# A hybrid RWKV-7 and convolution block: other waits, buffers, sums and lags in a planned order of work

## The chip, the cores and the metric

The kernel runs on one core of a Trainium2 chip. The metric is device time in microseconds; before the change the median of three runs is 1135.36 us (1134.06 to 1135.81). TensorE does the matrix products, ScalarE (ACT) activations and evictions from PSUM, VectorE (DVE) elementwise work, GpSimd (POOL) here mostly issues transfers, and SyncE (SP) issues the others.

## What is computed

One layer on 512 tokens with 1024 channels, all in float32. The input x is normalised and goes through one wide projection; its columns feed two branches, which are gated and merged, projected, and added to x; a gated feed-forward layer of width 2816 follows.

```python
h = rms_norm(x, pre_mix_norm); proj = h @ w_in
p_r, p_k, p_v, p_c, z_rwkv, z_conv = split(proj)
y_rwkv = rwkv7_time_mix(...)      # per token and head, S is 64x64:
#   sa = S a_t;  S = S * w_t + sa b_t' + v_t k_t';  y_t = S r_t
#   then a norm over each head, a bonus term, a gate and @ w_rwkv_out
y_conv = conformer_conv(p_c, ...) # u * sigmoid(gate), a causal depthwise
#   convolution of 31 taps, layer_norm, silu, @ w_conv_out
merged = sigmoid(z_rwkv) * y_rwkv + sigmoid(z_conv) * y_conv
x = x + rms_norm(merged @ w_out)
f = (silu(h2 @ ffn_w_gate) * (h2 @ ffn_w_up)) @ ffn_w_down
x = x + rms_norm(f)
```

## The kernel before

Channels lie on the 128 partitions, in eight tiles (ct = 0 to 7, two heads each), and the 512 tokens along the free dimension. Float32 products are made from two rounded parts: each factor is split into a high and a low part, and `acc3` makes three matmuls of 512 columns for each 128x128 block (high by high, high by low, low by high). A dense tile of the projection is 8 such blocks, 24 matmuls, in two halves of four blocks.

The weights of a half are loaded by `wload` (L437). In the usual way SP loads wf, ACT makes wh and DVE subtracts to get wl. In the way used during the time mixing, `eng is G`, GpSimd loads wh, ACT writes wl = -wh, and a second GpSimd transfer adds the weights to wl while it writes (`accum_op`), so that wl holds what the rounding left out. wh and wl share twelve buffers, that is six halves.

The time mixing is cut into 8 chunks of 64 tokens. For each tile four generators run, with their priorities: `prep` (2), `values` (2), `chain` (0), and `taps` (5); `solve` and `finish` are started by prep and chain (3).

- `prep(ct)` makes the keys, waits for inner(ct-1) and chain(ct-2), writes AR and bk, transposes bk, then waits for solve(ct-1) (L832) and makes the products gps between them, of which Mt is evicted. Then it posts inner(ct) and starts solve(ct).
- `solve(ct)` inverts the triangular 64x64 matrices in Mt: blocks of 16 on DVE (tt, Ps), and then the products wqs, xqs, wps and xps on TensorE. Its result goes into Pbd, of which there are two (ct % 2).
- `values(ct)` waits for the dense tile v and writes UV and SV (product vps), then the bonus (product bps), and posts val(ct). vps, bps and the four products of solve share one PSUM buffer, tag "sb", in the order in which they ask for it.
- `chain(ct)` waits for chain(ct-1), val(ct) and solve(ct), and goes through the 8 chunks in sequence: zt from AR and SV, eviction zs on ACT, zt from Pbd and zs, two evictions UV, zt from bkT and UV, two evictions SV, and the next chunk.
- `taps(ct)` adds the 31 taps of the convolution into csum_ on DVE, each operation reading the sum that the one before wrote (L1057).

The order on each engine is written by a planner, `Sched`, while the program is built. Every operation is put into a queue of its engine and stream, with its inputs, priority and estimated duration (`times`). `run` takes the operation that can start earliest by the planner's clocks; among those that can start within EPS = 0.15 us of that, the one of lowest priority number. `after` (L272) says when a result may be used on another engine: its end plus LAG of the engine that makes it. A generator that yields an event goes on when that event's operations have been issued in the plan. Dense tiles are the filler (priority 4); `feed` loads at most WB = 6 halves ahead, and each tile of the projection has events that it needs: v of tile ct needs val(ct-1), the convolution's columns from tile 5 on need inner(ct-1), the gates z_conv need inner(7) and val(7). The engines themselves run in order and wait only for semaphores, so an operation that the plan places late isn't run earlier, and a DMA whose buffer is free may be issued before the plan's time.

After the eighth chain come the output projections, the convolution's norm, the merge and the feed-forward layer; from the projection w_out on the order is that of the code, without the planner.

Of the kernel before, what the change touches and what calls it, by code (L numbers as in the profile page):

```python
# [9 lines left out]
F32 = mybir.dt.float32  # L10
F32R = mybir.dt.float32r
I32 = mybir.dt.int32
AF = mybir.ActivationFunctionType
ALU = mybir.AluOpType
# [3 lines left out]
P = 128  # L18
T = 512
# [4 lines left out]
NCH = T // L  # L24
# [5 lines left out]
KW = 31  # L30
# [2 lines left out]
WT = 4  # L33
LB = {"mu_r": 2, "mu_k": 2, "mu_v": 1}
NWO = 3
BUFS = (2, 2, 2, 2, 1, 1, 1)
EPS = 0.15
C0 = math.exp(-0.5)
RSQ = float(0x5F3759DF)
# [42 lines left out]
def tile_hybrid_block(ctx, tc, xT, cst, prm, dwp, wl1, w2g, w_in, w_ro, w_co, w_o,  # L82
# [13 lines left out]
    class Sched:  # L96
# [7 lines left out]


        ENGS = ("PE", "ACT", "DVE", "POOL", "SP")
        LAG = {"PE": 0.06, "ACT": 0.07, "DVE": 0.06, "POOL": 0.1, "SP": 0.1}

        def __init__(self):
            self.cur, self.pri, self.seq = None, 0, 0  # L110
# [71 lines left out]
        def times(self, eng, name, k, aps):  # L182

            out = aps[0]
            n = math.prod(out.shape[1:])
            if eng == "PE":
                lhsT, rhs = k["lhsT"], k["rhs"]
                n, m = math.prod(rhs.shape[1:]), math.prod(lhsT.shape[1:])
                if lhsT.dtype == F32R:
                    c = max(0.112, 0.452e-3 * n)  # L190
                elif name == "transpose":
                    c = 0.112
                elif m > 64:
                    c = 2 * (0.112 if n <= P else 1.02e-3 * n) * (0.52 if lhsT.shape[0] <= 64 else 1)
                else:
                    c = 0.058 if m > 32 else 0.016
                return c, c + 0.17, 0.0
            if "dma" in name:
                size = P * n * 4 if out.shape[0] > 64 else 64 * n * 4
                land = 2.0 + size / 200e3  # L200
                if eng == "POOL":
                    return (0.91, 0.06, land + 0.7) if k.get("accum_op") else (0.65, 0.06, land + 0.3)
                return 0.06, 0.06, land
            psum = any(str(a.space) == "PSUM" for a in aps[1:])
            if eng == "ACT":
                t = 0.17 + 0.9e-3 * n - (0.03 if psum else 0)
                t += sum(0.08 for a in ("scale", "bias") if hasattr(k.get(a), "ap"))
                return t + 0.02, t, 0.0
            if eng == "POOL":
                return 0.2 + 1.2e-3 * n, 0.2 + 1.2e-3 * n, 0.0  # L210
            t = 0.16 + 1.035e-3 * n
            if name == "scalar_tensor_tensor":
                t += 0.05 if n > 64 else 0
            elif name == "transpose":
                t = 0.16 + 1.8e-3 * n
            elif name == "tensor_tensor_scan":
                t = 0.16 + 2.06e-3 * n
            elif name in ("tensor_scalar", "tensor_copy"):
                t = 0.15 + 0.75e-3 * n
            return t - 0.08, t, 0.0  # L220
# [139 lines left out]
    sc = Sched()  # L360
# [18 lines left out]
    V, G, S = Engine("DVE", nc.vector), Engine("POOL", nc.gpsimd), Engine("ACT", nc.scalar)  # L379
    PE, SY = Engine("PE", nc.tensor), Engine("SP", nc.sync)  # L380
# [17 lines left out]
    def f(ap):  # L398
        return ap.bitcast(F32)
# [17 lines left out]
    def vec(name, ct, lo=0, hi=P):  # L417
        j = VECS.index(name) * NT + ct
        return pr[lo:hi, j:j + 1]
# [17 lines left out]
    def wload(wap, nk, eng=None):  # L437
        if eng is G:
            wh, wl = (wp.tile([P, nk * P], F32R, tag=f"w{next(turn) % 3}", name=n_)
                      for n_ in ("wh", "wl"))  # L440
            G.dma_start(out=wh, in_=wap)
            S.activation(out=wl, in_=f(wh), func=AF.Copy, scale=-1.0)
            with sc.stream("low"):
                G.dma_start(out=wl, in_=wap, accum_op=ALU.add)
        else:
            wf = wp.tile([P, nk * P], F32, tag="w0", name="wf")
            wh, wl = (wp.tile([P, nk * P], F32R, tag=f"w{i}", name=n_)
                      for i, n_ in ((1, "wh"), (2, "wl")))
            SY.dma_start(out=wf, in_=wap)
            split(wf, wh, wl)  # L450
        return wh, wl
# [78 lines left out]
    cpad0 = hp.tile([P, KW - 1 + T], F32, tag="cpad0", bufs=1, name="cpad0")  # L530
    G.memset(cpad0[:, 0:KW - 1], 0.0)
    csum_ = hp.tile([P, KW - 1 + T], F32, tag="cpad1", bufs=1, name="cacc")
# [32 lines left out]
    for k in range(NT):  # L565
        if k == WK:
# [4 lines left out]
                               op0=ALU.mult, op1=ALU.subtract)  # L571
# [11 lines left out]
    def normed():  # L583
        for k in range(NT):
# [7 lines left out]
                    op0=ALU.mult, op1=ALU.add)  # L592
# [3 lines left out]
                    op0=ALU.mult, op1=ALU.add)  # L596
# [3 lines left out]
    Pbd = []  # L600
    kp = None
# [71 lines left out]
    def open_loop():  # L673
        nonlocal kp
        ctx_e.close()
        kp = pool(ctx_w, "kp", 2)
        for j in range(2):
            t_ = kp.tile([P, NCH, P], F32, tag=f"Pbd{j}", bufs=1, name=f"Pbd{j}")
            G.memset(t_, 0.0)
            Pbd.append(t_)  # L680

    def ktmp(name, bufs=1, cols=T):
        pool = kp if name in ("mu_v", "ep") else kq
# [61 lines left out]
    def once(fn):  # L745
        fn()
        yield from ()


    def prep(ct):  # L750
# [9 lines left out]
        for R, c in ((E, slice(0, P)), (O, slice(P, 2 * P))):  # L760
# [8 lines left out]
                             op0=ALU.mult, op1=ALU.add)  # L769
# [29 lines left out]
                               op0=ALU.mult, op1=ALU.mult)  # L799
# [18 lines left out]
        for hc in range(2):  # L818
            ps = pm.tile([P, 4, P], F32, tag="sm", name="tps")
            for c in range(4):  # L820
# [6 lines left out]
                               op0=ALU.mult, op1=ALU.mult)  # L827
        sc.post(("tr", ct))


        if ct:
            yield ("solve", ct - 1)  # L832
        Mt = kp.tile([P, NCH, L], F32, tag="Mt", bufs=BUFS[4], name="Mt")
        GR = kp.tile([P, NCH, 2, L], F32, tag="GR", bufs=BUFS[1], name="GR")
        sm = lambda rows: m_str[rows].unsqueeze(1).to_broadcast([64, 4, L])
        for hc in range(2):
# [6 lines left out]
            for par, ps in enumerate(pss):  # L843
# [3 lines left out]
                             func=AF.Copy)  # L847
                S.activation(out=Mt[r0 + B32:r0 + L, cc, 0:B32],
                             in_=ps[r0 + B32:r0 + L, :, B32:L], func=AF.Copy)
# [3 lines left out]
        s_.update(AR=AR, GR=GR, bkT=bkT, dL=dL)  # L853
        sc.post(("inner", ct))
        s_.update(Mt=Mt)
        sc.spawn(once(lambda: solve(ct)), 3)

    def solve(ct):
        s_ = st[ct]
# [4 lines left out]
                    in_=Mt[:, :, 0:B32].rearrange("p c t -> p t c").unsqueeze(2)  # L864
# [7 lines left out]
        for j in range(B16 - 1, 0, -1):  # L872
            q0 = j // 4
            n = 4 - q0
# [6 lines left out]
                    in_=Ps[:, 0:B32 * 8].rearrange("p (i q) -> p q i", q=8))  # L881
# [28 lines left out]
                          start=True, stop=True)  # L910
        for h in range(2):
            S.activation(out=Wt[R2[h]], in_=ps[R2[h]], func=AF.Copy)
        pb = Pbd[ct % 2]
        for h in range(2):
            for j, R in enumerate((R1[h], R2[h])):
                S.activation(out=pb[R, :, h * L + j * B32:h * L + (j + 1) * B32], in_=P32[R],
# [111 lines left out]
    conv_in = {}  # L1028

    def conv_place(ct):  # L1030
        if "ca" not in acts:
            acts["ca"] = hp.tile([P, NT, KW - 1 + T], F32, tag="ca", name="ca")
            G.memset(acts["ca"][:, :, 0:KW - 1], 0.0)
        return acts["ca"][:, ct, :]
# [22 lines left out]
    def taps(ct):  # L1057
        tap = lambda j: dw[:, ct * KW + j:ct * KW + j + 1]
        yield ("cv", ct)
        if ct:  # L1060
            yield ("taps", ct - 1)
        else:
            yield "low1"
        cb, o_ = conv_in[ct], csum_[:, 0:T]
        V.tensor_scalar(out=o_, in0=cb[:, 0:T], scalar1=tap(0), scalar2=vec("conv_b", ct),
                        op0=ALU.mult, op1=ALU.add)
        for j in range(1, KW):
            to = o_ if j < KW - 1 else conv_place(ct)[:, KW - 1:]
            V.scalar_tensor_tensor(out=to, in0=cb[:, j:j + T], scalar=tap(j), in1=o_,
                                   op0=ALU.mult, op1=ALU.add)  # L1070
        sc.post(("taps", ct))
        if ct == NT - 1:
            sc.fast = False
# [380 lines left out]
```

## Time and profile before

| | |
|---|---|
| runs | 1135.81, 1134.06, 1135.36 us |
| profiled execution | 1134.7 us, span 1132.9 us |
| granted clock of TensorE, mean | 0.974 |
| busy: TensorE, DVE, ACT, POOL | 1080.3, 745.1, 573.8, 106.0 us |
| dense matmuls, name dn, from 75 to 530 us | 887, 256.0 us busy |
| chain that ended last, on PE | 84% of the span |

The span runs from the first to the last instruction of the profiled execution. Busy times are unions of the instructions of an engine. Matmuls are pipelined and their modelled lengths overlap, so the step from one to the next is read from the start times. The granted clock is a share: 1.00 is 2.4 GHz, 0.50 is 1.2 GHz.

### The profile page before, as it was taken

To read this page: it belongs to the slowest core of one execution; us is meant where nothing else is said; L and a number is where in the kernel's file an instruction comes from. 1 tells how busy PE (TensorE), PEld (TensorE's weight loads), DVE (VectorE), ACT (ScalarE), POOL (GpSimd) and SP (SyncE) were. 2 spreads that over 40 slices of the span, in tenths; PEclk is the share of its full clock that TensorE was granted. 3 is DMA by queue.
4 is the path that set the end of the run, shared out by engine and by line. 5 is a ranking of instruction groups with operands and counts; after the bars stand their busy time and mean duration, and the time that the engine had idled before them with its cause. 6 is when DMAs were issued, how large, how long until landed. Compare 5 with 4: busy or idle time off the path is not lost.

```text
span 1132.9 us, 18576 instructions
## 1 busy us (share of the span) xinstructions
PE 1080.3 (95%) x7066; PEld 865.5 (76%) x7066; DVE 745.1 (66%) x1503; ACT 573.8 (51%) x1199; POOL 106.0 (9%) x175
## 2 busy tenths in 40 slices
PE   7799999998999999979999999999999999999996
PEld 5587777776676777757878888898888888888886
DVE  5878989898888898988855257375444444433324
ACT  5556677777666676545366235453333333333321
POOL 0013322131231221110000000000000000000000
PEclk9899999999998999969999999999999999999998
DMA  6117755262545344343322225401222222333312
GB/s 235 38 38 149 150 110 115 54 128 45 109 74 121 74 108 78 76 68 114 107 84 96 93 93 168 130 1 56 94 93 93 93 95 97 96 96 103 113 53 75
DMA packets 69017, 108.01 MB, mean 95 GB/s; under 512 B 15168, under 2 KB 20672, under 8 KB 68928
## 3 DMA queue, kind: packets, MB, share of 16 engines
q1 hardware_dynamic: 48768, 70.11, 19.8%
q0 software_dynamic: 20160, 36.71, 16.3%
q8 instruction: 56, 0.92, 0.3%
q14 instruction: 33, 0.27, 0.1%
HBM read 102.60 MB, written 2.10 MB: 92 GB/s over the span
## 4 chain that ended last, share of the span: by engine, by line
PE 84%; issue 7%; DVE 4%; ACT 2%; DMA 1%; POOL 1%; SPq 0%; DVEq 0%; POOLq 0%; ACTq 0%
PE dn L225 35%; PE dn L300 29%; PE zt L300 5%; PE lora L300 2%; PE psf L225 2%; PE gps L300 2%; PE wo L225 2%; PE yp L300 1%; PE vps L300 1%; PE psn L225 1%; PE tps L300 1%; POOL wl L300 1%; ACT Mt L300 1%; PE ssy L300 1%; POOL wh L300 0%
## 5 line engine op out<-in xcount | busy, mean ns | idle before, releaser
L225 ACT ACTIVATE wh<-wf 128x512 fp32r<-128x512 f32 x140 | 86.7, 619 | 217.8 <-PE dn L225 207.3
L225 DVE TENSOR_TENSOR wl<-wf,wh 128x512 fp32r<-128x512 f32 x140 | 94.2, 674 | 123.8 <-ACT wh L225 123.7
L300 PE MATMUL dn<-HH,wl 128*128 128x512 f32 x408 | 167.9, 412 | 3.0 <-DMA wl<-in_w_in_dram 3.0
L300 PE MATMUL dn<-HL,wh 128*128 128x512 f32 x408 | 168.4, 413 | 0.0
L300 PE MATMUL dn<-HH,wh 128*128 128x512 f32 x408 | 167.7, 411 | 0.0
L300 DVE SCALAR_TENSOR_TENSOR cacc<-ca,dw,cacc 128x512 f32<-128x512 f32 x203 | 151.9, 748 | 4.9
L225 PE MATMUL dn<-FHH,wl 128*128 128x512 f32 x320 | 127.7, 399 | 0.0
L225 PE MATMUL dn<-FHL,wh 128*128 128x512 f32 x320 | 126.2, 394 | 0.0
L225 PE MATMUL dn<-FHH,wh 128*128 128x512 f32 x320 | 125.5, 392 | 0.0
L225 PE MATMUL dn<-FH,wh 128*128 128x512 f32 (+1 forms) x332 | 101.3, 388 | 0.0
L300 PEld LDWEIGHTS dn<-HH,wl 128*128 128x128 f32 x408 | 78.2, 192 | 17.7 <-DMA wl<-in_w_in_dram 3.6
L300 PEld LDWEIGHTS dn<-HH,wh 128*128 128x128 f32 x408 | 78.1, 192 | 14.4 <-issue 0.2
L300 PEld LDWEIGHTS dn<-HL,wh 128*128 128x128 f32 x408 | 78.1, 191 | 14.2 <-issue 0.5
L300 POOL DMA_DIRECT2D wl<-in_w_in_dram x70 | 61.8, 931 | 262.9 <-ACT wl L300 188.4
L300 ACT ACTIVATE wh<-wf 128x512 fp32r<-128x512 f32 x68 | 42.3, 628 | 74.0 <-PE dn L300 69.4
L225 PEld LDWEIGHTS dn<-FH,wh 128*128 128x128 f32 x332 | 61.5, 188 | 13.9
L225 PEld LDWEIGHTS dn<-FHL,wh 128*128 128x128 f32 x320 | 60.1, 188 | 15.6
L300 DVE TENSOR_TENSOR wl<-wf,wh 128x512 fp32r<-128x512 f32 x68 | 46.5, 688 | 38.2 <-ACT wh L300 38.0
L225 PEld LDWEIGHTS dn<-FHH,wh 128*128 128x128 f32 x320 | 60.1, 188 | 14.3
L225 PEld LDWEIGHTS dn<-FHH,wl 128*128 128x128 f32 x320 | 60.1, 188 | 13.7
L225 PE MATMUL dn<-FH,wl 128*128 128x512 f32 (+1 forms) x166 | 64.0, 385 | 0.0
L300 POOL DMA_DIRECT2D wh<-in_w_in_dram x70 | 45.6, 718 | 36.9 <-PE dn L300 36.1
(304 smaller groups left out, 2078.6 us busy)
## 6 DMA issues: line engine op xcount, KB each, us to landing
wh<-in_w_in_dram POOLq DMA_DIRECT2D x70, 256.0 KB, 5.1
wl<-in_w_in_dram POOLq DMA_DIRECT2D x70, 256.0 KB, 4.4
wf<-in_w_gt_dram SPq DMA_DIRECT2D x44, 256.0 KB, 2.7
wf<-in_w_up_dram SPq DMA_DIRECT2D x44, 256.0 KB, 2.6
wf<-in_w_in_dram SPq DMA_DIRECT2D x42, 256.0 KB, 2.9
wf<-in_w_dn_dram SPq DMA_DIRECT2D x40, 256.0 KB, 2.7
wf<-in_w_ro_dram SPq DMA_DIRECT2D x16, 256.0 KB, 2.6
wf<-in_w_co_dram SPq DMA_DIRECT2D x16, 256.0 KB, 2.7
```

Source lines behind the costliest of these rows:

```text
L225: return fn(*a, **k)
L300: i = fn(*a, **k)
```

## The change

It has five parts, all in the stretch that the planner orders.

1. The planner's lags grow: 0.15 us behind an operation of PE, ACT and DVE (0.06, 0.07 and 0.06 before) and 0.2 behind POOL (0.1). Elementwise work on POOL is priced at 0.2 us + 2 ns an element of a partition instead of 1.2 ns.
2. Mt has two buffers instead of one, and the products gps of tile ct wait for solve(ct-2) instead of solve(ct-1).
3. Pbd has one buffer instead of two. solve becomes a generator: after wps it waits for chain(ct-1), and then writes Pbd and makes xps.
4. In `wload` the negation wl = -wh moves from ACT to GpSimd, into the stream "low" beside the accumulating transfer.
5. For tiles 1 to 7 the taps go by turns into two sums, csum_ and cpad0 (the input of tile 0's convolution, not used after that), and one addition joins them.

```diff
-BUFS = (2, 2, 2, 2, 1, 1, 1)
+BUFS = (2, 2, 2, 2, 2, 1, 1)
...
-        LAG = {"PE": 0.06, "ACT": 0.07, "DVE": 0.06, "POOL": 0.1, "SP": 0.1}
+        LAG = {"PE": 0.15, "ACT": 0.15, "DVE": 0.15, "POOL": 0.2, "SP": 0.1}
...
             if eng == "POOL":
-                return 0.2 + 1.2e-3 * n, 0.2 + 1.2e-3 * n, 0.0
+                return 0.2 + 2e-3 * n, 0.2 + 2e-3 * n, 0.0
...
             G.dma_start(out=wh, in_=wap)
-            S.activation(out=wl, in_=f(wh), func=AF.Copy, scale=-1.0)
             with sc.stream("low"):
+                G.tensor_scalar(out=wl, in0=f(wh), scalar1=-1.0, scalar2=None, op0=ALU.mult)
                 G.dma_start(out=wl, in_=wap, accum_op=ALU.add)
...
-        for j in range(2):
-            t_ = kp.tile([P, NCH, P], F32, tag=f"Pbd{j}", bufs=1, name=f"Pbd{j}")
-            G.memset(t_, 0.0)
-            Pbd.append(t_)
+        t_ = kp.tile([P, NCH, P], F32, tag="Pbd", bufs=1, name="Pbd")
+        G.memset(t_, 0.0)
+        Pbd.append(t_)
...
-        if ct:
-            yield ("solve", ct - 1)
+        if ct > 1:
+            yield ("solve", ct - 2)
...
-        sc.spawn(once(lambda: solve(ct)), 3)
+        sc.spawn(solve(ct), 3)
...
-        pb = Pbd[ct % 2]
+        if ct:
+            yield ("chain", ct - 1)
+        pb = Pbd[0]
...
-        cb, o_ = conv_in[ct], csum_[:, 0:T]
-        V.tensor_scalar(out=o_, in0=cb[:, 0:T], scalar1=tap(0), scalar2=vec("conv_b", ct),
+        cb = conv_in[ct]
+        sums = [t_[:, 0:T] for t_ in ((csum_, cpad0) if ct else (csum_,))]
+        n = len(sums)
+        V.tensor_scalar(out=sums[0], in0=cb[:, 0:T], scalar1=tap(0), scalar2=vec("conv_b", ct),
                         op0=ALU.mult, op1=ALU.add)
-        for j in range(1, KW):
-            to = o_ if j < KW - 1 else conv_place(ct)[:, KW - 1:]
-            V.scalar_tensor_tensor(out=to, in0=cb[:, j:j + T], scalar=tap(j), in1=o_,
-                                   op0=ALU.mult, op1=ALU.add)
+        if n > 1:
+            V.tensor_scalar_mul(sums[1], cb[:, 1:1 + T], tap(1))
+        for j in range(n, KW):
+            V.scalar_tensor_tensor(out=sums[j % n] if j < KW - 1 or n > 1 else
+                                   conv_place(ct)[:, KW - 1:], in0=cb[:, j:j + T],
+                                   scalar=tap(j), in1=sums[j % n], op0=ALU.mult, op1=ALU.add)
+        if n > 1:
+            V.tensor_add(conv_place(ct)[:, KW - 1:], *sums)
```

## Rows read from the trace of the kernel before

**Rows 1.** The page, part 1: busy us (share of the span) and instructions.
```profile
PE 1080.3 (95%) x7066; PEld 865.5 (76%) x7066; DVE 745.1 (66%) x1503; ACT 573.8 (51%) x1199; POOL 106.0 (9%) x175
```

**Rows 2.** Stretches: length, busy us and count by engine, granted clock, DMA share, GB/s.
```profile
75.00:530.00 455.00, 429.33 (x4024) 331.60 (x4023) 397.94 (x921) 301.87 (x751) 102.52 (x161) 0.95 0.46 95
...
100.00:275.00 175.00, 171.50 (x1741) 133.35 (x1740) 158.88 (x393) 122.88 (x300) 43.83 (x69) 1.00 0.50 102
275.00:400.00 125.00, 114.23 (x1047) 88.93 (x1048) 108.24 (x236) 83.70 (x207) 30.62 (x49) 0.92 0.48 101
...
475.00:525.00 50.00, 40.98 (x244) 30.44 (x243) 39.42 (x66) 28.32 (x76) 5.18 (x6) 0.80 0.32 65
525.00:1133.00 608.00, 596.40 (x2832) 491.00 (x2830) 299.37 (x515) 231.95 (x386) 0.00 (x0) 0.99 0.30 93
```

**Rows 3.** The seven stretches at a clock of 0.50 to 0.51, summed, by engine.
```profile
sum 41.10, PE 36.56 PEld 29.71 DVE 32.20 ACT 20.45 POOL 8.37; mean PE 5.22 PEld 4.24 DVE 4.60 ACT 2.92 POOL 1.20
```

**Rows 4.** The same seven stretches, the instructions of tile dn alone.
```profile
sum 41.10, PE 11.37 PEld 7.14 DVE 0.00 ACT 0.00; mean PE 1.62 PEld 1.02 DVE 0.00 ACT 0.00
```

**Rows 5.** A stretch of dense matmuls alone, at full clock.
```profile
600.00:625.00 25.00, 25.00 (x109) 20.17 (x108) 12.25 (x20) 14.33 (x21) 0.00 (x0) 1.00 0.32 108
```

**Rows 6.** Timeline of PE, 355 to 361 us: start, us, engine, line, operation, idle before.
```profile
356.46 0.49 PE L300 MATMUL zt<-SV,AR 128*128 128x128 f32 x2 [0.36 <-ACT SV L300]
...
359.80 0.49 PE L300 MATMUL zt<-SV,AR 128*128 128x128 f32 x2 [0.72 <-ACT SV L300]
```

**Rows 7.** Tile zt, who waited for it: us in all, times.
```profile
  PE zt L300: 13.3, 24
```

**Rows 8.** Timeline of ACT, 338 to 348 us: the last copies into Pbd.
```profile
345.67 0.76 ACT L300 ACTIVATE Pbd<-xps 32x256 f32<-32x256 f32 x2
```

**Rows 9.** Timeline of PE, 338 to 348 us: the products gps of the next tile.
```profile
346.69 0.48 PE L300 MATMUL gps<-AR,bk 64*128 64x128 f32 x2
```

**Rows 10.** Tile Pbd: durations in ns, least, median and most; first and last start.
```profile
L300 ACT ACTIVATE Pbd<-P x32: 397/415/417, 126.3 to 475.5; 32x256 f32<-32x256 f32 x32
L300 ACT ACTIVATE Pbd<-xps x16: 373/375/377, 128.6 to 478.8; 32x256 f32<-32x256 f32 x16
L300 POOL MEMSET Pbd<- x2: 962/962/962, 67.1 to 68.0; 128x1024 f32 x2
```

**Rows 11.** Timeline of ACT, 470 to 486 us: the last v tile's eviction.
```profile
476.50 0.69 ACT L300 ACTIVATE mu_v<-dn,drv 128x512 f32<-128x512 f32 x1
```

**Rows 12.** Timeline of PE, 476 to 496 us: values, bonus, first dense matmul after them.
```profile
481.03 2.08 PE L300 MATMUL vps<-cs,mu_v 128*128 128x128 f32 x8
...
490.99 0.77 PE L300 MATMUL dn<-HH,wh 128*128 128x512 f32 x1
```

**Rows 13.** Groups by line and shape: count, busy us, mean ns, idle before.
```profile
L300 ACT ACTIVATE wl<-wh 128x512 fp32r<-128x512 f32 x70 | 43.3, 627 | 1.8 <-DMA wh<-in_w_in_dram 0.6
```

**Rows 14.** Timeline of POOL, 455 to 496 us.
```profile
458.12 3.22 POOL L300 DMA_DIRECT2D wh<-in_w_in_dram  x6
491.07 0.89 POOL L300 DMA_DIRECT2D wl<-in_w_in_dram  x1 [29.73 <-ACT wl L300]
```

**Rows 15.** Waits of PE: for whom, us in all, times, longest.
```profile
PE dn L300 <- DMA wl<-in_w_in_dram: 3.0, 2, 2.3
```

**Rows 16.** Timeline, 494 to 504 us: eight taps on DVE without a break.
```profile
493.91 6.26 DVE L300 SCALAR_TENSOR_TENSOR cacc<-ca,dw,cacc 128x512 f32<-128x512 f32 x8
```

**Rows 17.** Timeline of DVE, 67 to 70 us: two operations that don't read each other.
```profile
68.71 0.75 DVE L300 SCALAR_TENSOR_TENSOR mu_k<-dn,pr,mu_k 128x511 f32<-128x511 f32 x1
69.37 0.68 DVE L300 TENSOR_TENSOR wl<-wf,wh 128x512 fp32r<-128x512 f32 x1
```

**Rows 18.** Tile cacc: the first tap, durations in ns.
```profile
L300 DVE TENSOR_SCALAR cacc<-ca,dw,pr x7: 541/545/546, 137.5 to 504.7; 128x512 f32<-128x512 f32 x7
```

**Rows 19.** Timeline of ACT, 576 to 584 us: the normed convolution, first tile.
```profile
582.74 0.62 ACT L300 ACTIVATE CH<-ca 128x512 fp32r<-128x512 f32 x1
```

**Rows 20.** Timeline of PE, 650 to 656 us: the first matmul that reads it.
```profile
652.71 0.40 PE L300 MATMUL dn<-CH,wh 128*128 128x512 f32 x1
```

## The prediction

> **What bounds the kernel now.** I read the page's shares first: TensorE is busy 1080.3 us, 95% of the span of 1132.9 [rows 1]. Then I cut the span into stretches, to see where the other 52 us lie and at what clock [rows 2]. After 525 us some 12 us of 608 are idle, at a granted clock of 0.99: the end of the kernel is TensorE work that this change does not touch. From 75 to 530 us, in the part that the planner orders, TensorE is busy 429.3 of 455.0, so 25.7 us are idle, at a mean clock of 0.95. By parts, 100 to 275 us has 3.5 us idle; 275 to 400 us has 10.8 (clock 0.92), and 475 to 525 us has 9.0 (clock 0.80). TensorE is the limit while it has dense work, and loses time where the recurrence alone may run.
>
> The clock is the second loss. Seven short stretches, 41.1 us together, ran at 0.50, the lower level of 1.2 GHz, each behind an idle time. TensorE is busy 36.6 us in them, 11.4 of it in dense matmuls [rows 3, 4]. A dense matmul takes 0.229 us at the higher level (25.00 us for 109) [rows 5] and twice that at the lower, so half of the 11.4 is lost, 5.7 us. Of the other 25.2 busy us between none and half is the clock's; I take a quarter, 6. So about 12 us (6 to 18) go with the clock. Idle time and clock together are 37 us (32 to 44), and that is all that another order can win in this stretch.
>
> DVE comes next: 397.9 us of the 455, 87%; in 100 to 275 us it is 158.88 of 175, 91%. ACT has 301.9 (66%), POOL 102.5 (23%) [rows 2].
>
> **The change part by part.** The profiled execution took 1134.7 us, 1.8 more than its span and 0.7 less than the median of 1135.36; the sum is made against 1134.7.
>
> *Margin (LAG).* One step of the recurrence without dense work takes 3.34 us, from zt at 356.46 to zt at 359.80 us [rows 6]. By the prices and lags in its code the planner sets 3.04 us for these six hops (PE 0.45, zs 0.33, PE 0.45, UV 0.49, two products 0.68, SV 0.65, lags included); the new lags add three times 0.09 and three times 0.08 and make it 3.55. So the old plan calls a step ready 0.3 us early, and TensorE, which works in order, stands there; the new one is 0.2 late, and dense matmuls fill that. All that TensorE's matmuls wait for evictions of zt and of what follows it is 13.3 us, 24 times [rows 7], partly where no dense matmul is at hand, as in the step of [rows 6]. So margin alone wins between 0 and 8 us, and may lose 3 by starting late what could start; I take a win of 2.
>
> *Second Mt, one Pbd, the new waits.* With two buffers for Mt the products gps of tile ct need no finished solve(ct-1). In tile 5 this wait decides: the last copies of solve(4) start at 345.67 and take 0.76, and gps follows at 346.69 [rows 8, 9]. In exchange solve(ct) writes its result only after chain(ct-1): four copies of 0.415 us, then two of 0.375 [rows 10], 2.4 us on ACT, ahead of the first product with it. Queued behind them on ACT are the next chain's evictions and the prep of the tile after. Where that is late, it costs 2.4 us a tile in 7 tiles, 17 us; where the preceding chain ends before the values are ready, nothing. The new wait also turns the order on the one PSUM buffer "sb": the values' product vps stood behind xps of the same tile, and may now come ahead of it. This matters most at the end: mu_v of the last tile is evicted at 476.50, vps starts at 481.03, and only when the values are done may the next gate tiles be loaded; the first dense matmul follows at 490.99 [rows 11, 12]. In the 50 us around it TensorE loses 9.0 us idle and some 6 by clock. I take 7 of these 15 as won, and 6 of the 16 in 275 to 400 us (10.8 idle, 5 by clock). The ends are all 31 won, and 17 lost.
>
> *Negation on GpSimd.* ACT loses 70 activations, 43.3 us [rows 13], 14% of its work in the stretch. That is off the path, but it ends a wait: POOL issues six wh loads from 458.12 us on, and then stands 29.73 us for ACT's copy, which lies far back in ACT's order, until wl's DMA at 491.07 [rows 14]. TensorE's own wait for wl is 3.0 us [rows 15]; it goes, and is counted in the idle time above. What one negation takes on POOL no row shows. Below it lies half of the 0.962 us memset of 1024 columns, 0.48; above it one such memset for reading and writing 512 columns and a wait for a whole tap of 0.75, 1.7 [rows 10, 16]. I take 1.0, nearer to the memset. POOL then has 102.5 + 70 = 172 us (136 to 222) of 455. Behind the negation in POOL's queue stand the wl DMA of the same half and the wh DMAs of the halves that follow; with over half of POOL idle they come no later than they are used.
>
> *Taps in two sums.* Eight taps in a row take 6.26 us, 0.783 each; two operations that don't read each other start 0.66 apart (68.71 and 69.37) [rows 16, 17]. Per tile 0.545 + 30 x 0.783 = 24.0 us become 2 x 0.545 + 29 x 0.66 + 0.68 = 20.9 (0.545 is the first tap's [rows 18], 0.68 the TENSOR_TENSOR's of [rows 17]): 3.1 us by seven tiles, 22 us where all follow each other, some 12 where a part lies between other work. TensorE gets nothing from it: the first CH made from the taps is written at 582.74 and read at 652.71 us, 70 us later [rows 19, 20].
>
> *DVE against GpSimd.* POOL's two memsets [rows 10] only write, and POOL has no operation that reads SBUF, so the trace leaves open whether a negation and a tap can run together. If not, DVE pays 70 x 0.48 to 0.96, 34 to 67 us; if they can, nothing. I take 15, about what the two sums return, and so no cost on the path. The Trainium skill ("SBUF — State Buffer", section "SBUF: two separate sides") speaks against the change here: a DVE operation with two SBUF inputs and a GpSimd operation that reads SBUF take one port pair in turn, each for its whole length. No run here shows it yet. By that rule the 34 to 67 would be paid, and the first rival below is what that makes of the time.
>
> Sum: 1134.7 - 2 - 7 - 6 = 1119.7, and at the level of the median 1120.
>
> **The rivals.**
> *GpSimd stops DVE (slower).* DVE has 398 + 50 (the middle of 34 to 67) - 15 = 433 us. It decides from 413 us on, 91% of the 455, the highest share in [rows 2]. At that share 433 us need 476, 21 more than now, less some 6 that TensorE still wins: 1150 (1138 to 1165). For: DVE is 87% full, and most of its work there reads two tensors. Against: the taps may end 70 us later before anybody waits for them.
> *The starvation stays (no change).* The gates' loads still wait for the values of the last tile, the recurrence still runs alone at 475 to 525 us, and a new order loses elsewhere what it wins: 1128 to 1137. For: the waits in the code that hold these loads back are the same. Against: the order on "sb" and the wait for solve are what make the values late.
> *One Pbd makes the chains wait (slower).* 17 us, less 3 won: 1149. It decides if solves are early and the chains follow each other at once. Against: the copies of solve(4) are followed by gps, not by the chain [rows 8, 9], so the values are what chains wait for.
> *All of it goes.* Idle time and half-speed stretches vanish but for a few us: 1100 (1095 to 1106).
>
> **How the numbers follow.** My forecast, 1106 to 1129, gets 0.49; GpSimd against DVE 0.21; no change 0.17; one Pbd 0.07; all of it 0.06. 0.2% is 2.3 us, about what a measurement of this kernel can tell from no change. Of the no-change case 0.09 falls within it, 0.06 is faster, 0.02 slower. So faster is 0.49 + 0.06 + 0.06 = 0.61, same 0.09, slower 0.21 + 0.07 + 0.02 = 0.30. For 8 in 10 the range reaches from 1101 to 1151: left out are half of the two slow cases, 0.14, and half of the fastest, 0.03. The likeliest case's own range is 1106 to 1129.
>
> **What would show it.** The margin: TensorE's waits behind zt below 10 us in all. The new waits: under 6 us idle in 275 to 400 us, and the last chain with dense matmuls between its steps and the clock at its higher level. POOL: wl's DMAs a few us behind the landing of wh, and no wait of 20 us for them. The sums: taps 0.66 apart. Against me: taps of 1 us and more beside negations, negations far above 1 us, or DVE over 413 us in the stretch; a chain that starts right behind Pbd's copies while TensorE idles; a new idle stretch of TensorE at another place.

## The result, and the profile after

The changed kernel takes 1142.0 us (median of four runs, 1141.9 to 1142.9) against 1135.6 for the kernel before on the same chip: a ratio of 1.0056, 95% interval 1.0035 to 1.0076. It is slower by 0.6%, where 1120 was forecast.

The page's busy times, as in [rows 1]; the span is 1141.1 us:

```profile
PE 1076.2 (94%) x7066; PEld 871.9 (76%) x7066; DVE 759.8 (67%) x1511; ACT 533.0 (47%) x1130; POOL 218.8 (19%) x241
```

TensorE is busy 4.1 us less and idle 12.3 us longer (64.9 against 52.6): the span is 8.2 longer. DVE is busy 14.7 us longer, although the two sums were to save it 15. The stretches, with the columns of [rows 2], tell where the idle time is:

```profile
75.00:530.00 455.00, 417.40 (x3958) 331.03 (x3957) 407.37 (x911) 255.02 (x670) 216.23 (x228) 0.94 0.44 90
100.00:275.00 175.00, 162.36 (x1511) 129.31 (x1515) 157.75 (x363) 96.42 (x246) 101.22 (x107) 0.96 0.53 109
275.00:400.00 125.00, 114.92 (x1280) 91.54 (x1276) 113.29 (x264) 80.47 (x210) 53.02 (x56) 0.95 0.41 81
400.00:475.00 75.00, 68.80 (x621) 55.42 (x619) 66.17 (x162) 40.35 (x114) 38.27 (x44) 0.95 0.52 110
475.00:525.00 50.00, 42.52 (x412) 32.49 (x410) 47.16 (x79) 22.06 (x68) 15.04 (x12) 0.80 0.27 51
```

From 75 to 530 us TensorE is idle 37.6 us, 25.7 before. Most of the new idle time lies from 100 to 275 us, where it was 3.5 and is 12.6; 400 to 475 us has 6.2 (1.9 before), and 275 to 400 us has 10.1 (10.8 before). The chain that ended last, shares by engine, before and after, has 18% on DVE, where it had 4%:

```profile
PE 84%; issue 7%; DVE 4%; ACT 2%; DMA 1%; POOL 1%; SPq 0%; DVEq 0%; POOLq 0%; ACTq 0%
...
PE 69%; DVE 18%; ACT 3%; DMA 2%; issue 2%; DVEq 0%; ACTq 0%
```

What TensorE's matmuls wait for in the kernel after (us in all, times, longest), the view of [rows 15]:

```profile
PE zt L300 <- DMA SV<-UV: 8.3, 4, 2.6
...
PE gps L300 <- DVE AR L300: 4.1, 2, 2.9
PE zt L300 <- ACT SV L300: 3.4, 6, 0.7
...
PE wqs L300 <- DVE n L300: 2.0, 1, 2.0
PE vps L300 <- DVE mu_v L300: 2.0, 1, 2.0
```

The wait for wl is gone; waits for DVE have come (AR, n, mu_v). Added up over this view's lines of the planned part (L300), TensorE waits 12.6 us for DVE, 2.3 before. The wait for the transfer that completes the values (SV<-UV) was 0.7 us before; what makes it late is not shown.

One of the waits for DVE can be followed back. vps of the last tile, at 481.03 in [rows 12], starts at 491.69:

```profile
491.69 1.39 PE L300 MATMUL vps<-cs,mu_v 128*128 128x128 f32 x8 [2.00 <-DVE mu_v L300]
```

```profile
484.81 1.83 DVE L300 SCALAR_TENSOR_TENSOR cacc<-ca,dw,cacc 128x512 f32<-128x512 f32 x1
...
488.56 1.09 DVE L300 SCALAR_TENSOR_TENSOR cacc<-ca,dw,cacc 128x512 f32<-128x512 f32 x1
...
490.90 0.74 DVE L300 SCALAR_TENSOR_TENSOR mu_v<-dn,pr,mu_v 128x511 f32<-128x511 f32 x1
```

ACT's part of mu_v is done at 488.96, but DVE's part stands behind taps until 490.90. DVE works without a break there, and four of its operations from 481.71 us on, beside negations, are 2.1 us longer in all than undisturbed ones: about what vps waits. That vps is 10.7 us later than in [rows 12] has mostly another cause: the dense tile v itself comes later (ACT's eviction of mu_v is at 488.27, and at 476.50 in [rows 11]).

The group that took the place of [rows 13] (busy us, mean ns, idle before):

```profile
L300 POOL TENSOR_SCALAR wl<-wh 128x512 fp32r<-128x512 f32 x69 | 122.8, 1780 | 83.0 <-DMA wh<-in_w_in_dram 49.5 <-PE dn L300 23.4 <-issue 6.4
```

A negation takes 1.78 us by the mean, above my upper bound of 1.7. What DVE does beside it is seen in two stretches of the timelines, POOL's first (start, us, operation):

```profile
112.00 1.83 POOL L300 TENSOR_SCALAR wl<-wh 128x512 fp32r<-128x512 f32 x1
...
181.36 4.12 POOL L300 TENSOR_SCALAR wl<-wh 128x512 fp32r<-128x512 f32 x1 [1.01 <-DMA wh<-in_w_in_dram]
...
287.95 1.83 POOL L300 TENSOR_SCALAR wl<-wh 128x512 fp32r<-128x512 f32 x1
```

```profile
111.73 1.26 DVE L300 TENSOR_TENSOR tt<-Mo,Ps 128x30 f32<-128x30 f32 x1
113.03 0.19 DVE L300 TENSOR_TENSOR Ps<-Ps,tt 128x30 f32<-128x30 f32 x1
...
182.06 0.73 DVE L300 SCALAR_TENSOR_TENSOR cacc<-ca,dw,cacc 128x512 f32<-128x512 f32 x1
182.73 0.73 DVE L300 SCALAR_TENSOR_TENSOR cpad<-ca,dw,cpad 128x512 f32<-128x512 f32 x1
...
287.15 0.74 DVE L300 SCALAR_TENSOR_TENSOR cpad<-ca,dw,cpad 128x512 f32<-128x512 f32 x1
287.81 1.63 DVE L300 SCALAR_TENSOR_TENSOR cacc<-ca,dw,cacc 128x512 f32<-128x512 f32 x1
```

An operation of solve that takes 0.19 us takes 1.26 beside the negation at 112.00; a tap of 0.74 takes 1.63 beside the one at 287.95. At 181.36 it is the other way round: taps follow each other 0.66 us apart, undisturbed, and the negation takes 4.12 us. So the two engines hold each other up.

Here they don't do so for the negation's whole length. A negation, and two operations of solve beside it, each with two inputs in SBUF:

```profile
270.83 1.49 POOL L300 TENSOR_SCALAR wl<-wh 128x512 fp32r<-128x512 f32 x1 [1.44 <-DMA wh<-in_w_in_dram]
```

```profile
270.90 0.59 DVE L300 TENSOR_TENSOR Ps<-Ps,tt 128x36 f32<-128x36 f32 x1
271.52 0.19 DVE L300 TENSOR_TENSOR tt<-Mo,Ps 128x30 f32<-128x30 f32 x1
```

The first of them ends 0.66 us after the negation's start. The second, and the two that follow it, take their usual 0.18 to 0.19 us while the negation is recorded as running until 272.32; the profile gives GpSimd's spans only roughly.

### The profile page after: what moved, and what is told of

Its sections match the earlier page's. It is cut to its first block, busy times and chain, and to the rows that moved or that the text cites. A ratio compares the mean times of both kernels' runs of the same rounds, so it can differ in the third digit from the quotient of the medians.

```text
span 1141.1 us, 18557 instructions
## 1 busy us (share of the span) xinstructions
PE 1076.2 (94%) x7066; PEld 871.9 (76%) x7066; DVE 759.8 (67%) x1511; ACT 533.0 (47%) x1130; POOL 218.8 (19%) x241
## 4 chain that ended last, share of the span: by engine, by line
PE 69%; DVE 18%; ACT 3%; DMA 2%; issue 2%; DVEq 0%; ACTq 0%
PE dn L225 33%; PE dn L300 21%; PE zt L300 4%; DVE cacc L300 4%; DVE cpad L300 2%; PE psf L225 2%; DMA SV<-UV 2%; PE wo L225 2%; DVE Ps L300 2%; DVE tt L300 2%; PE gps L300 1%; PE lora L300 1%; PE yp L300 1%; DVE AR L300 1%; DVE ry L300 1%
## 5 line engine op out<-in xcount | busy, mean ns | idle before, releaser
L300 PE MATMUL dn<-HL,wh 128*128 128x512 f32 x408 | 171.0, 419 | 0.5 <-issue 0.5
L300 PE MATMUL dn<-HH,wl 128*128 128x512 f32 x408 | 170.3, 417 | 0.0
L300 PE MATMUL dn<-HH,wh 128*128 128x512 f32 x408 | 169.8, 416 | 0.0
L300 POOL TENSOR_SCALAR wl<-wh 128x512 fp32r<-128x512 f32 x69 | 122.8, 1780 | 83.0 <-DMA wh<-in_w_in_dram 49.5
L300 PEld LDWEIGHTS dn<-HH,wl 128*128 128x128 f32 x408 | 79.2, 194 | 14.9 <-issue 1.3
L300 PEld LDWEIGHTS dn<-HH,wh 128*128 128x128 f32 x408 | 79.0, 194 | 14.9 <-issue 1.0
L300 PEld LDWEIGHTS dn<-HL,wh 128*128 128x128 f32 x408 | 79.1, 194 | 14.4 <-issue 0.5
L300 DVE SCALAR_TENSOR_TENSOR cacc<-ca,dw,cacc 128x512 f32<-128x512 f32 x105 | 84.4, 804 | 0.0
L300 ACT ACTIVATE wh<-wf 128x512 fp32r<-128x512 f32 x69 | 42.7, 627 | 75.5 <-PE dn L300 70.8
L300 DVE SCALAR_TENSOR_TENSOR cpad<-ca,dw,cpad 128x512 f32<-128x512 f32 x98 | 75.5, 770 | 0.0
L225 PEld LDWEIGHTS dn<-FHL,wh 128*128 128x128 f32 x320 | 60.1, 188 | 15.7
L300 DVE TENSOR_TENSOR wl<-wf,wh 128x512 fp32r<-128x512 f32 x69 | 47.3, 689 | 36.3 <-ACT wh L300 33.8
L300 POOL DMA_DIRECT2D wl<-in_w_in_dram x69 | 62.6, 907 | 23.0 <-POOL wl L300 19.9
```

Of the source, the lines that this page charges most:

```text
L225: return fn(*a, **k)
L300: i = fn(*a, **k)
```

## The experiments

Ratios are to the kernel before in the same session, whose median was 1134.1 to 1137.1 us, with 95% intervals.

| kernel | what it is | median us | ratio (95%) |
|---|---|---|---|
| no_pool | changed, negation on ACT | 1112.7 | 0.978 (0.9754 to 0.9805) |
| no_lag | changed, old lags | 1145.5 | 1.0073 (1.0046 to 1.01) |
| no_buf | changed, old buffers and waits | 1149.0 | 1.0102 (1.0074 to 1.013) |
| no_taps | changed, one sum | 1146.8 | 1.0083 (1.0054 to 1.0113) |
| no_pool_lag | as no_pool, old lags | 1123.7 | 0.9909 (0.9891 to 0.9926) |
| no_pool_buf | as no_pool, old buffers | 1124.9 | 0.991 (0.9883 to 0.9937) |
| no_pool_taps | as no_pool, one sum | 1120.3 | 0.9873 (0.9856 to 0.9889) |
| order_before_pool | order of before, negation run by GpSimd | 1157.9 | 1.0212 (1.0182 to 1.0242) |
| order_after_act | order of after, negation run by ACT | 1121.1 | 0.9877 (0.9857 to 0.9897) |
| memset_order_before | order of before, GpSimd writes wl, hardly reads | 1141.1 | 1.006 (1.0034 to 1.0086) |
| half_order_before | the same, half of the reading | 1141.6 | 1.0066 (1.0041 to 1.0092) |
| memset_after | changed, GpSimd writes wl, hardly reads | 1129.8 | 0.9959 (0.9935 to 0.9983) |
| true_price | changed, negation priced 1.79 us | 1150.7 | 1.0151 (1.0129 to 1.0173) |
| charged | the same, and DVE charged 0.38 us | 1149.2 | 1.0123 (1.0093 to 1.0154) |
| dve_unplanned | before, 140 additions on DVE outside the plan | 1142.2 | 1.0062 (1.0038 to 1.0085) |
| dve_planned | before, such additions inside the plan | 1136.7 | 1.0022 (1.0002 to 1.0043) |
| act_taps | as no_pool, first product of each sum on ACT | 1109.9 | 0.978 (0.9762 to 0.9798) |

Several times fell outside the ranges that the theories gave. no_pool came out faster than any of them had it, and order_before_pool slower; memset_order_before, memset_after, dve_unplanned, no_pool_taps and act_taps lie between the ranges of their theories, and true_price above both of its own.

**Which part costs.** Each part of the change was undone by itself. The edit of no_pool (the planner's price of POOL's elementwise work goes back as well; without the negation it bears on memsets only):

```diff
             G.dma_start(out=wh, in_=wap)
+            S.activation(out=wl, in_=f(wh), func=AF.Copy, scale=-1.0)
             with sc.stream("low"):
-                G.tensor_scalar(out=wl, in0=f(wh), scalar1=-1.0, scalar2=None, op0=ALU.mult)
                 G.dma_start(out=wl, in_=wap, accum_op=ALU.add)
```

> The changed kernel with the negation back on ACT; lags, buffers and taps as changed. Theory A (a negation on GpSimd and a DVE operation of two SBUF inputs take turns, 26 us of DVE time in the trace of the changed kernel, and that makes late what the plan calls ready): the time falls from 1142 to 1124 to 1134, below before, and no DVE tap is over 0.8 us. Theory B (the longer lags stretch the eight chains): still 1138 to 1144. Theory C (one Pbd): still 1138 to 1144.

> The changed kernel with the lags of before. Theory A: 1138 to 1146, since DVE is still stopped by the negations. Theory B: 1130 to 1136, with chains of 28 us instead of 30 to 35. Theory C: no change, 1140 to 1144.

> The changed kernel with one Mt, two Pbd and the old waits around solve. Theory A: 1140 to 1148, as the wins of the earlier solve are lost as well. Theory B: 1140 to 1146. Theory C: 1132 to 1137, and the last chain starts right behind its values.

> The changed kernel with the taps in one sum. Theory A: 1143 to 1150, since DVE loses some 15 us of what the two sums returned. A theory D, that taps which overlap keep a negation waiting (one of 4.1 us in the trace): 1136 to 1140, and no negation above 2.4 us. Theory B and C: 1140 to 1144.

Only with the negation back on ACT is the kernel faster, by 2.2%; the other three parts undone leave it where it is or make it slower still. So neither the longer lags, nor the two sums, nor the buffers with their waits are what costs. One Pbd by itself, with the second Mt kept, was not undone. The page's busy times of no_pool (span 1112.2 us), and its stretch of 75 to 530 us:

```profile
PE 1063.5 (96%) x7066; PEld 862.1 (78%) x7066; DVE 731.5 (66%) x1511; ACT 568.1 (51%) x1197; POOL 103.6 (9%) x172
```

```profile
75.00:530.00 455.00, 434.49 (x4121) 345.45 (x4120) 408.18 (x966) 307.59 (x767) 101.00 (x159) 0.98 0.46 100
```

DVE has 13.6 us less than before the change; 10.5 of it are the two sums' (742.0 in no_pool_taps). TensorE's waits for DVE in the planned part are 2.2 us in all, 2.3 before the change. TensorE is idle 20.5 us in the stretch at a clock of 0.98.

**The same order, another engine.** The change also makes the planner put everything else in another order. To keep the order and change the engine alone, the plan is made for one engine and the instruction issued on the other:

```diff
+            sc.swap = "POOL"
+            neg = S.activation(out=wl, in_=f(wh), func=AF.Copy, scale=-1.0)
+            neg.call = (nc.gpsimd.tensor_scalar, (), dict(out=wl, in0=f(wh), ...))
+            sc.swap = None
```

> The kernel before, with its planned order of PE, DVE, ACT and SP kept instruction by instruction; only the negation is executed on GpSimd, at its place in the plan, and ACT has 70 instructions fewer. Theory A (GpSimd and DVE take turns, and DVE's late results stop TensorE): slower than before by 5 to 15 us, 1141 to 1151, with DVE operations of 0.2 us stretched to 1 us beside negations. Theory E (the new order around GpSimd's negation is what costs, not the turns): no slower than before, 1130 to 1136, since ACT is freed and TensorE's 3 us of waits for wl go.

> The changed kernel with its planned order kept; only the negation is executed on ACT, at the place where the plan has it on GpSimd, so ACT has 69 instructions more than its plan allows for. Theory A: faster than the changed kernel's 1142, 1122 to 1134, though ACT is a little late. Theory E: 1140 or more, as the order is the same and ACT is burdened.

In the order of the kernel before, GpSimd's negation costs 2.1%, 24 us; in the order of the changed kernel, ACT's in its place wins 1.8%. So the order alone is not the cause, though it has a part: no_pool, whose plan knows that ACT negates, is another 1.0% faster. Busy times of order_before_pool, and how long two small operations of DVE took there (ns: least, median, most; they take 206 and 173 at most in the kernel before):

```profile
PE 1085.4 (94%) x7066; PEld 867.9 (75%) x7066; DVE 774.7 (67%) x1503; ACT 533.7 (46%) x1129; POOL 221.4 (19%) x245
```

```profile
L301 DVE TENSOR_TENSOR tt<-Mo,Ps x120: 166/191/1018, 104.7 to 485.8; 128x24 f32<-128x24 f32 x24, 128x30 f32<-128x30 f32 x16, 128x36 f32<-128x36 f32 x16, 128x28 f32<-128x28 f32 x8
...
L301 DVE TENSOR_SCALAR ry<-n x16: 171/172/1739, 76.8 to 551.8; 128x8 int32<-128x8 int32 x16
```

DVE is busy 29.6 us longer than in [rows 1], with the same 1503 instructions. ry has one input in SBUF and is held as well, and for the whole negation:

```profile
362.38 1.83 POOL L301 TENSOR_SCALAR wl<-wh 128x512 fp32r<-128x512 f32 x1
```

```profile
362.50 1.74 DVE L301 TENSOR_SCALAR ry<-n 128x8 int32<-128x8 int32 x1
```

The negation ends at 364.21 and ry at 364.24.

**The price by itself.** Behind the kernel before, negations and taps on tiles of their own, then taps into two sums, one-input operations and memsets (its time is longer by them and means nothing):

```diff
+    negs(6)
+    for i in range(16):
+        stt(s0, s2)
...
```

> The kernel before with six groups of operations put behind its last output (its time is longer by these and says nothing): 6 negations of 128x512 on GpSimd alone; beside 16 DVE taps that each read the sum of the one before (two SBUF inputs); beside 16 taps in two sums; beside 16 DVE operations of one SBUF input; beside 16 taps of which one input is in PSUM; and 6 memsets beside 16 taps. Theory A: a negation alone takes 0.5 to 0.9 us, beside taps of two SBUF inputs 1.5 us or more, and some of these taps 1.1 to 1.6 us instead of 0.75; beside the PSUM taps and for the memsets both are undisturbed. Theory E: a negation takes 1.5 us alone as well and no tap is stretched.

The timeline of POOL, and DVE's beside it:

```profile
1122.22 1.49 POOL L225 TENSOR_SCALAR pdst<-psrc 128x512 fp32r<-128x512 f32 x1 [20.60 <-DVE fl L225]
...
1172.27 0.53 POOL L225 MEMSET pdst<- 128x512 f32 x1
...
1174.36 0.79 POOL L225 MEMSET pdst<- 128x512 f32 x1
```

```profile
1131.37 0.68 DVE L225 SCALAR_TENSOR_TENSOR q<-q,q 128x512 f32<-128x512 f32 x1
...
1132.09 0.98 DVE L225 SCALAR_TENSOR_TENSOR q<-q,q 128x512 f32<-128x512 f32 x1
...
1147.38 0.41 DVE L225 TENSOR_SCALAR q<-q 128x512 f32<-128x512 f32 x1
...
1148.73 0.69 DVE L225 TENSOR_SCALAR q<-q 128x512 f32<-128x512 f32 x1
1149.34 1.08 DVE L225 SCALAR_TENSOR_TENSOR q<-q,q 128x512 f32<-128x512 f32 x1
```

A negation takes 1.49 us with hardly anything beside it: my 1.0 was too little whatever DVE does. A tap of 0.68 us takes 0.98 to 1.08 beside one. The groups of operations slid into each other, so taps that read PSUM beside negations were not measured.

**Reading, or GpSimd's own length?** GpSimd's negation is also longer than ACT's (1.78 against 0.63 us), and GpSimd's queue waits behind it. Here GpSimd negates one column, or 256, and then writes wl, or its other half, three times, which reads nothing from SBUF:

```diff
+    i = nc.gpsimd.tensor_scalar(out=out[:, 0:1], in0=in0[:, 0:1], scalar1=-1.0, ...)
+    for _ in range(3):
+        i = nc.gpsimd.memset(f(out)[:, 0:], 0.0)
```

> The order planned for the kernel before, in which a negation executed on GpSimd cost 2.1 % (1157.87 us). Here GpSimd negates one column only, so that it still waits for wh, and then writes wl three times with memsets, which do not read SBUF: some 1.7 us at the same place in the same queue, as long as the negation was. Left out: wl is then not what the rounding left out. Theory A (GpSimd's reading beside DVE costs DVE its time): the loss goes, 0.985 to 1.003 of the kernel before, 1117 to 1138 us, and taps beside it stay at 0.75 us. Theory N (GpSimd's own 1.75 us in place of ACT's 0.63, and what stands behind it in its queue, cost the time): 1.015 to 1.025, 1151 to 1163 us.

> The same, but GpSimd negates 256 of the 512 columns, and then writes the other 256 three times with memsets, about as long in all as the whole negation. Left out: half of wl's columns are not what the rounding left out. Theory A: half the reading costs half the time, 1.006 to 1.014, 1141 to 1150 us. Theory N: as with the whole negation, 1.015 to 1.025, 1151 to 1163 us.

> The changed kernel in its own order, with one column negated and three memsets in place of the negation. Left out: wl is not what the rounding left out. Theory A: as with the negation executed on ACT in this order (0.9877) or a little better, since ACT is free of it: 0.975 to 0.99, 1106 to 1123 us. Theory N: little better than the changed kernel, 0.998 to 1.006, 1132 to 1141 us.

Busy times and the taps' durations of memset_order_before, and what GpSimd did (busy us, mean ns):

```profile
PE 1083.3 (95%) x7066; PEld 868.9 (76%) x7066; DVE 745.4 (65%) x1503; ACT 533.9 (47%) x1129; POOL 248.0 (22%) x455
```

```profile
L301 DVE SCALAR_TENSOR_TENSOR cacc<-ca,dw,cacc x203: 706/752/756, 141.7 to 558.0; 128x512 f32<-128x512 f32 x102
```

```profile
L452 POOL MEMSET wl<- 128x512 f32 x210 | 110.6, 527 | 12.2
...
L446 POOL TENSOR_SCALAR wl<-wh 128x1 fp32r<-128x1 f32 x70 | 39.9, 570 | 69.4 <-PE dn L301 38.4 <-DMA wh<-in_w_in_dram 27.3 <-issue 3.4
```

GpSimd is held 2.15 us a half (0.570 + 3 x 0.527), longer than by the negation, and yet no tap that reads two tensors is over 0.756 us and DVE's busy time is that of [rows 1]. The loss falls from 2.12% to 0.60%. TensorE's waits for DVE in the planned part fall with it, from 12.2 to 3.6 us, and DVE's share of the chain that ended last from 17% to 8%. So 1.5%, 17 us, is what GpSimd's reading beside DVE costs, in an order that is the same, and the remaining 0.6%, 7 us, goes with the operation's being on GpSimd at all, its length and the queue behind it. Both theories hold a part, A the larger. In the order of the changed kernel the parts are 0.97% (1.0056 to 0.9959) and 0.82% (0.9959 to 0.9877). Since the memsets hold GpSimd longer than the negation did, the part of the length is rather less than this and that of the reading rather more. The trace of memset_after shows one way in which the length costs:

```profile
197.77 0.80 PE L300 MATMUL zt<-SV,AR 128*128 128x128 f32 x2 [6.86 <-POOL SV L300]
```

In this execution, of 1123.1 us, TensorE waits 6.86 us for GpSimd's zeroing of SV, ahead of which two halves stand in GpSimd's queue (from 188.91 us on). The trace of the changed kernel has no such wait, so in its own order 0.82% is probably too much for the length.

With half the columns read, DVE's busy time goes up by a third of what the whole negation adds, and the time hardly or not at all (1.0066 against 1.006; a third of the 1.5% would make it 1.011, beyond the interval's end of 1.0092):

```profile
PE 1079.4 (95%) x7066; PEld 864.5 (76%) x7066; DVE 755.2 (66%) x1503; ACT 533.5 (47%) x1129; POOL 242.7 (21%) x455
```

So between these runs the loss doesn't grow in step with DVE's time.

**What the other parts win.** With the negation on ACT, each of the three was undone:

> The changed kernel with the negation on ACT and the old buffers and waits around solve: lags and two sums alone. If the earlier solve is what wins (theory F): 1125 to 1135, most of the 24 us that the kernel without the GpSimd negation wins are lost. If the lags and the two sums win (theory G): 1112 to 1120.

> The changed kernel with the negation on ACT and the lags of before: buffers and two sums alone. If the longer lags win (theory G): 1118 to 1126. If they cost or do nothing, as theory B had it: 1106 to 1113.

> The changed kernel with the negation on ACT and the taps in one sum: lags and buffers alone. Theory H: DVE has 15 to 20 us more, 1125 to 1133. Theory I: 1111 to 1117.

Undoing the lags or the buffers costs 1.3% each, and undoing the two sums 0.9%. Their sum, 3.5%, is more than the 2.2% that all three win together. With the negation on GpSimd the same three edits are worth 0.2%, 0.5% and 0.3%, mostly within the intervals.

**Can the plan take it up?** The planner priced the negation at 1.22 us and knew nothing of DVE's loss. The first edit is in both kernels, the second in charged alone:

```diff
-                return 0.2 + 2e-3 * n, 0.2 + 2e-3 * n, 0.0
+                return 0.2 + 3.1e-3 * n, 0.2 + 3.1e-3 * n, 0.0
...
+            if e == "POOL" and o.busy > 1.5:
+                self.clock["DVE"] = max(self.clock["DVE"], t) + 0.38
```

> The changed kernel with the planner's price of the GpSimd negation raised from 1.22 to 1.79 us, about what one took in the trace of the changed kernel (1.78). Theory A (DVE loses its time whatever the plan holds of GpSimd): 1137 to 1147. Theory J (the plan is wrong on GpSimd's time, and a right price mends it): 1115 to 1130.

> The changed kernel with the negation still on GpSimd, and a planner that prices it at 1.79 us and adds 0.38 us to DVE's clock for each (26 us in the trace by 69). Theory K: the known loss costs less, 1120 to 1135. If the turns cannot be planned for, since the operation that is hit isn't the one that the plan charges (theory M): 1138 to 1150.

Both are slower than the changed kernel. So a plan with the true means is no better. That it would have to know which DVE operation is hit is a guess that no run tests.

**DVE time that the plan doesn't know.** Two additions of 30 columns on DVE were put with each of ACT's negations in the kernel before, unknown to the plan or in it (there 164, 30.5 us, reading wh):

```diff
+                for _ in range(2):
+                    d_ = nc.vector.tensor_tensor(out=csum_[:, T:], in0=cs[:, 0:30],
+                                                 in1=cs[:, 30:60], op=ALU.add)
```

> The kernel before, negation on ACT, its planned order kept; at each of the 70 negations two additions of 30 columns (0.19 us each, with the gap 0.45) are put into DVE's order without the planner's knowledge, 31 us of DVE time in all. Theory K (any DVE time that the plan doesn't know delays what TensorE waits for): 1148 to 1160, as with the negation on GpSimd in the same order (1158). Theory L (GpSimd does harm by something else, its own queue or the weights' lateness): 1134 to 1141.

> The kernel before with the same 140 additions as operations of the plan, behind the landing of wh. Theory K: the plan moves them to where DVE has room, 1134 to 1144. Theory H (a microsecond of DVE is one of time): 1148 to 1160.

```profile
PE 1083.5 (95%) x7066; PEld 866.0 (76%) x7066; DVE 760.8 (67%) x1643; ACT 573.7 (50%) x1199; POOL 105.7 (9%) x175
...
L446 DVE TENSOR_TENSOR cacc<-cs 128x30 f32<-128x30 f32 x140 | 26.0, 186 | 2.5
```

Outside the plan the additions, 26.0 us in all, raise DVE's busy time by 15.7 us (760.8 against 745.1) and cost 0.6%, 7 us; inside it they cost 0.2%. The stretched operations raise the busy time by 29.3 us (774.7 less the 745.4 of the memsets) and cost 17 us. That is 0.45 and 0.58 us of time for each microsecond of DVE. With intervals of 0.24% and more on each loss the two can't be told apart, and nothing here shows that a stretched operation costs more than other DVE time that the plan doesn't know. The run with half of the reading, 9.8 us of DVE for 0.06%, fits neither rate well. Busy times are of one execution each.

Added up by group, DVE's operations are 30.7 us longer beside the negations than beside the memsets. The taps have 12.1 of it; the rest lies on other operations, many of them the short dependent ones of solve and of the norms (tt, ry above). Whether those cost more than the taps was not tested.

**Less DVE work still.**

```diff
-        V.tensor_scalar(out=sums[0], in0=cb[:, 0:T], scalar1=tap(0), ...)
+        S.activation(out=sums[0], in_=cb[:, 0:T], func=AF.Identity, scale=tap(0), ...)
```

> The kernel with lags, buffers and two sums of the change and the negation on ACT (1112.7), and with the first operation of each sum moved from DVE to ACT: DVE has 15 operations of 0.545 us fewer, 8 us, and ACT 15 of about 0.75 more, 11 us. Theory H (DVE is as much a limit of this stretch as TensorE, so that a microsecond of DVE is about one of time): 1102 to 1108. Theory I (DVE has room, and only what the negations make late at single places costs): 1111 to 1115.

The ratio is that of no_pool: DVE's 7.7 us less (723.8 against 731.5) win nothing that shows. ACT is busy 12.1 us longer for it (580.2 against 568.1), so a small gain may be hidden. act_taps and no_pool are the fastest versions, 2.2% below the kernel before and some 2.7% below the changed one.

## Why the prediction was wrong

The direction was wrong, and the step that failed is "DVE against GpSimd": "I take 15, about what the two sums return, and so no cost on the path".

- The size. The exclusion was left open in [rows 10] and is there: DVE pays 23 us in the changed kernel (759.8 against 736.7 with memsets), 0.33 a negation, and 29 in the order of before. My value was 15; the lower bound of 34 was too high. It gave each negation 0.48 us of DVE at least, and the mean is 0.33 to 0.42; the operation beside the negation at 270.83 loses 0.39 (0.59 against 0.20).
- The reasoning. What DVE pays was set off against what the two sums save, and both put beside the path because the taps are read 70 us later. That is true of the taps and not of DVE. It works in order, and behind a stretched tap stand mu_v, AR, n and solve, which TensorE waits for: 12.6 us in all, where it was 2.3. The same error made me price the two sums at nothing: 0.66 us from tap to tap came as worked out, and where the negation is on ACT they are worth 0.9%. They save DVE 10.5 us, a little less than my 12 to 22.
- The negation itself: 1.0 forecast, 1.49 alone and 1.78 in the kernel, beyond the upper bound of 1.7. POOL has 216 us in the stretch, within 136 to 222. I held its length to be covered by POOL's idle time; by the runs with memsets, which are longer, it costs 0.6 to 0.8% at most. In the trace of memset_after one wait of 6.86 us for GpSimd's queue is most of that; which waits of the changed kernel belong to it stays open.
- The rival "GpSimd stops DVE" had the right sign and a range that holds the time (1138 to 1165). Its mechanism was right and its arithmetic was not: it put DVE at 433 us and let the time follow from DVE's share; the loss came with DVE at 407 us in the stretch, below the 413 from which it was to decide, and half the reading took a third of DVE's price and nothing of the time. A part of the loss was GpSimd's own length, which that rival left out.
- The Trainium skill ("SBUF — State Buffer", section "SBUF: two separate sides") spoke against the change, and was right that the two exclude each other. It says for the whole instruction. Here the operation held at 270.90 us goes on 0.66 us after the negation's start, and the next ones, each with two inputs in SBUF, take their usual time while the negation is recorded for another 0.83 us. So the trace agrees on the exclusion, and for operations with two inputs in SBUF not on its length; ry, with one, was held until the negation's end in order_before_pool. By the mean a negation of 1.78 us costs DVE 0.33.
- Margin: the waits for zt fell, as said, below 10 us (13.3 in [rows 7]):

```profile
  PE zt L300: 7.4, 15
```

  The wait for the transfer SV<-UV, which that row does not count, rose from 0.7 to 8.3 us. With the negation on ACT the margin is worth 1.3%, some 15 us, where 2 was taken and 8 the most.
- Buffers and waits: 13 us forecast, 1.3%, some 15 us, with the negation on ACT: right, and "under 6 us idle in 275 to 400 us" would have held there. In the changed kernel 10.1 are left, 5.8 of them waits for DVE (AR 2.9, n 2.0, ya 0.6, ys 0.3), and the clock from 475 to 525 us stays at 0.80, as before; in no_pool it is 0.97. The case in which one Pbd makes the chains wait is not borne out: with two of them, and one Mt, the kernel is no faster.
- POOL's wait of 20 us and TensorE's wait for wl went, as said.

In all, the three other parts win 2.2%, 25 us, where 15 was taken, and the negation on GpSimd costs 2.8%, 31 us (0.978 to 1.0056), where nothing was. 1.8% of that remains if the order is held (0.9877 to 1.0056); the rest belongs to what the planner makes of knowing ACT's negation.

## What to carry to other kernels

An engine that works in order is on the path as soon as anything in its queue is, even if most of its work is read much later: price a stretched operation by what stands behind it. Before an operation is moved to GpSimd because that engine is idle, ask what DVE does meanwhile, and test it with a GpSimd operation of the same length that doesn't read. When a change has several parts, undo each of them alone: three of these were worth 2.2%, and the fourth hid them.

## What the runs showed of the hardware

- A GpSimd TENSOR_SCALAR that reads SBUF and a DVE operation with two SBUF inputs exclude each other, for a part of the negation's length: at 270.83 us for the first 0.66 of 1.49 us, as recorded. Either can lose: a DVE operation of 0.19 us took 1.26, and a negation 4.12 while taps of two sums overlapped.
- DVE operations with one SBUF input can be held too: ry of 0.17 us took 1.74 in order_before_pool, until the negation beside it ended, and such operations of 0.41 us took 0.69 beside negations in the price run.
- GpSimd's memsets leave taps with two inputs alone (0.756 us at most). Beside one-input DVE operations of the price run a memset of 0.53 us took 0.79.
- Negating one column on GpSimd takes 0.57 us by the mean in memset_order_before and 0.21 at least; 512 columns take 1.49 alone.
